# Placing w_down's stationary operands at two residues modulo 256 bytes

## The chip, the cores and the metric

One core of a Trainium2 chip runs the whole program. The metric is the device time of one execution in microseconds (us). Each number below comes from the runs of the kernel before, from the profile of one execution of it, or from the addresses that the program's allocator gives to its tiles.

## The reference, cut to what matters

One layer of a decoder on 256 positions of width 1024, all float32. First a mixer of three attention branches, then a gated channel mixer ("the MLP half"), on which the change bears:

```python
h2 = rmsnorm(x, ln2)
u = causal_dwconv(h2 @ w_up, conv_w, conv_b)   # w_up: 1024 x 5632
a, b = jnp.split(u, 2, axis=-1)
return x + (jax.nn.silu(a) * b) @ w_down       # w_down: 2816 x 1024
```

A final RMSNorm with weight `ln_f` follows.

## The kernel before, in words

**Products in three parts.** Each float32 operand of a large product is split into a high part (rounded to the type float32r) and a low part (what the rounding left), and a product is the sum of three matmuls: high by high, low by high, high by low. `mm3` (line 241) issues them in this order for a stationary operand `lhs` and a moving operand `rhs`: `lh` with `rh` (line 243), `ll` with `rh` (line 244), `lh` with `rl` (line 245). Each matmul brings its own load of 128 stationary columns, which TensorE's load queue (PEld in the profile) works on while the matmul before it runs.

**Weights.** `Weights` (line 56) streams the weight pieces of 128 x 1024 from memory by the SP queue, in the order of use, into five raw buffers. Its step "hi" (line 109, ScalarE) makes `whi`, its step "lo" (line 116, VectorE) `wlo`. Six buffers of each lie in the pool `wpool`, and four more of each in the pool `mlp` during the MLP half.

**The MLP half** (from line 882) runs over j = 0 to 21, 128 channels of each half of `u` at a time. For each j:

- two w_up products, `up` (line 850) and `up_mm` (line 830), 24 matmuls each: the weights are the stationary operand, `h2T` (the normed input, transposed, 128 x 256 per step) is the moving one; line 834 issues all of them. Their results go to the PSUM banks `s0` and `s1` for even j, `pt` and `o` for odd j;
- `conv_of` (line 837) on VectorE and ScalarE for each of the two, SiLU (line 889), the product `pr` (line 894), and its split into `ah` (line 901) and `al` (line 902), each 128 x 256;
- from j = 2 on, save j = 9 and 16, one w_down product for an older j, `down` (line 823): `ah` and `al` are stationary, 128 columns at a time, and `whi` and `wlo` of w_down are moving, 512 wide. It is four calls of `mm3`, so 12 matmuls. `downs_after` (line 43) gives the plan: d = 0 at j = 2 up to d = 17 at j = 21. The last four d (18 to 21) come behind the loop, and the last columns of them in matmuls 256 wide.

The instructions stand in each engine's queue in the order in which the code issues them (`manual_schedule`), so the order on TensorE is: w_up, w_up, w_down, w_up, w_up, w_down, and so on. `ah` and `al` have a ring of six buffers each (`TAIL + 2`), so that slot j % 6 is written again six steps later.

**Names in the profile.** A group such as `acc<-whi,ah` names the output bank, the moving operand and the stationary operand in this order. `h2T` has the buffers of the earlier `oThi` and `oTlo`, so w_up reads `s<-oThi,whi`: moving `h2T` high, stationary `whi`. A PSUM tag's number is left out, so `s` is `s0` and `s1`.

**Addresses.** Modulo 256 bytes, within a partition:

| tile | where it is used | residue |
|---|---|---|
| `whi`, `wlo`, all ten buffers of each | stationary in w_up, moving in w_down, in w_o, in the branch projections | 64 |
| `oThi`, `oTlo` (later `h2T`) | stationary in the branch projections (`project`, line 701), moving in w_up | 0 |
| `hThi`, `hTlo` (later `mT`) | stationary in w_o (`wo_mm`, line 740) and in the row products of the attention half (`row_piece`, line 398), moving in `qk_piece` (line 378) | 64 |
| `v`, `ya`, `yb`, `pr` | the conv and its product | 64 |
| `ah`, `al`, six buffers of each | stationary in w_down | 64 |

Steps inside these tiles are multiples of 512 bytes, but for the row products 260 wide, so the residue of a tile is that of its slices.

Of the kernel before, what the change touches and what calls it, by code (L numbers as in the profile page):

```python
# [7 lines left out]
F32 = mybir.dt.float32  # L8
F32R = mybir.dt.float32r
# [3 lines left out]
P = 128  # L13
S = 256
# [18 lines left out]
TAIL = 4  # L33
# [9 lines left out]
def downs_after():  # L43

    out, d = [], 0
    for j in range(NF):
        if j >= 2 and j not in PAUSES:
            out.append(d)
            d += 1
        else:  # L50
            out.append(None)
    assert d == NF - TAIL
    return out
# [86 lines left out]
def hybrid_kernel(ctx: ExitStack, tc: tile.TileContext, x, xT, ln_f, w_main, w_v1, w_v2, b_f, sinks,  # L140
# [22 lines left out]
    def piece(lead=LEAD):  # L163
        nxt[0] += 1
        return W.use(nxt[0] - 1, lead, 1)
# [81 lines left out]
    def small(shape, name, bufs=2):  # L247
        return act.tile([P] + shape, F32, name=name, tag=name, bufs=bufs)
# [439 lines left out]
    ml = ctx.enter_context(tc.tile_pool(name="mlp", bufs=1))  # L688
# [124 lines left out]
    def up_banks(j):  # L813
        return [bank(tag, S) for tag in (("s0", "s1"), ("pt", "o"))[j % 2]]
# [8 lines left out]
    def down(j, parts):  # L823
        if not zo:
            zo.extend([bank("acc", 512, 4) for _ in range(2)] for _ in range(2))
        for t in range(2):
            for half in range(2):
                down_mm(j, t, half * 512, half * 512 + 512, parts)
# [8 lines left out]
    def conv_of(u, f, name):  # L837
        v = ml.tile([P, S], F32, name="v", tag="v", bufs=4)
        nc.vector.tensor_mul(v, u, rs["row2"])  # L839
        y = ml.tile([P, S], F32, name=name, tag=name, bufs=3)  # L840
        w = [cv[:, i * 2 * NF + f:i * 2 * NF + f + 1] for i in range(4)]
        nc.scalar.activation(y, v, AF.Identity, scale=w[2], bias=w[3])  # L842
        ahead()
        nc.vector.scalar_tensor_tensor(y[:, 1:S], v[:, 0:S - 1], w[1], y[:, 1:S],
                                       op0=OP.mult, op1=OP.add)
        nc.vector.scalar_tensor_tensor(y[:, 2:S], v[:, 0:S - 2], w[0], y[:, 2:S],
                                       op0=OP.mult, op1=OP.add)
        return y

    def up(j, c, u):  # L850
        parts = piece(0)
        for k in range(KD):
            up_mm(u, parts, k)

    def up_first(u):
        parts = [piece(0), piece(0)]
        for c in range(2):
            for k in range(4):
                up_mm(u[c], parts[c], k)
            if c == 0:  # L860
                low = h2_T(*blocks[-1], "pt")
                low()
                squares(*blocks[-1])
        rs["row2"], *finish = across(rstd_of(ss2[:, :, 0], ss2[:, :, 1], "n"), "row2", "acc", 4)
        ahead()
        for some in ((0, 1), (2,)):
            for k in range(4, KD):
                up_mm(u[0], parts[0], k, some)
        for k in range(4, KD):
            up_mm(u[1], parts[1], k)  # L870
        for f in finish:
            f()
        ahead()
        nc.scalar.preload_act_table_set("silu_and_others")

    def ahead():
        n = HL_BUFS + MORE_BUFS - 2
        W.prep_to(min(nxt[0] + n - 1, W.n_lo + 1))
        W.hi_to(min(nxt[0] + n, W.n_hi + 1))

    downs = downs_after()
    for j in range(NF):
        u = up_banks(j)
        if j == 0:
            up_first(u)
        else:
            up(j, 0, u[0])
        ya = conv_of(u[0], j, "ya")
        nc.scalar.activation(ya, ya, AF.Silu)
        if j:  # L890
            up(j, 1, u[1])
        yb = conv_of(u[1], j + NF, "yb")
        pr = ml.tile([P, S], F32, name="pr", tag="pr", bufs=3)
        nc.vector.tensor_mul(pr, ya, yb)
        hi = ml.tile([P, S], F32R, name="ah", tag="ah", bufs=TAIL + 2)
        lo = ml.tile([P, S], F32R, name="al", tag="al", bufs=TAIL + 2)
        d = downs[j]
        if d is not None:
            parts = piece(0)
            ahead()  # L900
        nc.scalar.activation(hi, pr, AF.Copy)
        nc.vector.tensor_sub(lo, pr, hi.bitcast(F32))
        mid[j] = (hi, lo)
        if d is not None:
            down(d, parts)
# [51 lines left out]
    v, r = (small([1], n) for n in ("fv", "fr"))  # L957
# [88 lines left out]
```

## Time and profile before

| | us |
|---|---|
| median of 3 runs | 388.01 (387.05 to 389.1) |
| the profiled execution | 388.68 |
| its span, first to last instruction | 387.0 |

The mean granted TensorE clock of the profiled execution is 0.993 of full speed. In the profile, PE is TensorE's matmuls, PEld its weight loads, DVE VectorE, ACT ScalarE, POOL GpSimd, SP the queue of SyncE that issues the transfers. The chain of work that ended last is followed back from the last instruction; in its list each entry has a start, a length and, for merged instructions of one line, their count. Matmuls overlap in their pipeline, so the "mean ns" of one in a group is longer than the distance from one start to the next; the distance is what the chain's lengths show, and it is what time is made of on TensorE.

### The profile page before, as it was taken

To read this page: it belongs to the slowest core of one execution; us is meant where nothing else is said; L and a number is where in the kernel's file an instruction comes from. 1 tells how busy PE (TensorE), PEld (TensorE's weight loads), DVE (VectorE), ACT (ScalarE), POOL (GpSimd) and SP (SyncE) were. 2 spreads that over 40 slices of the span, in tenths; PEclk is the share of its full clock that TensorE was granted. 3 is DMA by queue.
4 is the path that set the end of the run, shared out by engine and by line. 5 is a ranking of instruction groups with operands and counts; after the bars stand their busy time and mean duration, and the time that the engine had idled before them with its cause. 6 is when DMAs were issued, how large, how long until landed. Compare 5 with 4: busy or idle time off the path is not lost.

```text
span 387.0 us, 6530 instructions
## 1 busy us (share of the span) xinstructions
PE 377.2 (97%) x2464; PEld 340.1 (88%) x2464; DVE 287.7 (74%) x540; ACT 230.7 (60%) x399; POOL 8.0 (2%) x20
## 2 busy tenths in 40 slices
PE   6999999999999999999999999999999999999993
PEld 6999999787887888888899999999999999999983
DVE  3785967574856717967778999878887878888745
ACT  4883464665757685336587767556655656656433
POOL 4010000000000000000000000000000000000000
PEclk9899999999999999999999999999999999999998
DMA  7999765344552637444736567655565556463002
GB/s 197 402 331 334 279 181 181 130 130 149 170 172 90 218 108 233 151 160 119 262 108 222 204 224 223 216 196 186 170 213 180 201 171 205 171 218 109 2 0 108
DMA packets 21374, 70.86 MB, mean 183 GB/s; under 512 B 2504, under 2 KB 3413, under 8 KB 21344
## 3 DMA queue, kind: packets, MB, share of 16 engines
q1 hardware_dynamic: 20448, 68.05, 52.1%
q0 software_dynamic: 752, 2.18, 1.7%
q8 instruction: 19, 0.31, 0.4%
q10 hardware_dynamic: 144, 0.23, 0.2%
q14 instruction: 11, 0.09, 0.1%
HBM read 69.38 MB, written 1.07 MB: 182 GB/s over the span
## 4 chain that ended last, share of the span: by engine, by line
PE 96%; DMA 1%; DVE 1%; SPq 0%; ACT 0%; issue 0%; DVEq 0%
PE s L834 16%; PE acc L243 16%; PE acc L244 15%; PE acc L245 15%; PE pt L834 8%; PE o L834 8%; PE acc L394 7%; PE pt L394 2%; PE s L619 2%; PE o L394 1%; DMA raw<-in_w_main 1%; PE s L566 1%; PE s L608 1%; PE s L301 0%; PE pt L566 0%; PE pt L773 0%
## 5 line engine op out<-in xcount | busy, mean ns | idle before, releaser
L116 DVE TENSOR_TENSOR wlo<-raw,whi 128x1024 fp32r<-128x1024 f32 (+4 forms) x131 | 150.3, 1161 | 17.4 <-ACT whi L109 17.4
L109 ACT ACTIVATE whi<-raw 128x1024 fp32r<-128x1024 f32 (+4 forms) x131 | 129.1, 1005 | 49.2 <-PE acc L244 24.6
L243 PE MATMUL acc<-whi,hThi 128*128 128x512 f32 (+2 forms) x160 | 61.3, 383 | 0.0
L244 PE MATMUL acc<-whi,hTlo 128*128 128x512 f32 (+2 forms) x160 | 59.8, 374 | 0.0
L245 PE MATMUL acc<-wlo,hThi 128*128 128x512 f32 (+2 forms) x160 | 59.8, 374 | 0.0
L834 PE MATMUL s<-oThi,whi 128*128 128x256 f32 x176 | 49.3, 281 | 0.0
L834 PE MATMUL s<-oThi,wlo 128*128 128x256 f32 x176 | 49.2, 280 | 0.0
L834 PE MATMUL s<-oTlo,whi 128*128 128x256 f32 x176 | 48.9, 280 | 0.0
L842 ACT ACTIVATE ya<-v,cv 128x256 f32<-128x256 f32 x22 | 13.3, 603 | 42.7 <-DVE v L839 42.7
L243 PEld LDWEIGHTS acc<-whi,hThi 128*128 128x128 f32 x160 | 30.1, 188 | 6.0 <-issue 1.3
L245 PEld LDWEIGHTS acc<-wlo,hThi 128*128 128x128 f32 x160 | 30.0, 188 | 5.1
L244 PEld LDWEIGHTS acc<-whi,hTlo 128*128 128x128 f32 x160 | 30.1, 188 | 4.7 <-DVE hTlo L295 0.2
L244 PE MATMUL acc<-whi,al 128*128 128x512 f32 (+1 forms) x88 | 33.8, 384 | 0.0
L245 PE MATMUL acc<-wlo,ah 128*128 128x512 f32 (+1 forms) x88 | 33.8, 384 | 0.0
L243 PE MATMUL acc<-whi,ah 128*128 128x512 f32 (+1 forms) x88 | 33.8, 384 | 0.0
L834 PEld LDWEIGHTS s<-oTlo,whi 128*128 128x128 f32 x176 | 33.5, 191 | 0.0
L834 PEld LDWEIGHTS s<-oThi,wlo 128*128 128x128 f32 x176 | 33.0, 188 | 0.4
L834 PEld LDWEIGHTS s<-oThi,whi 128*128 128x128 f32 x176 | 33.0, 188 | 0.4
L834 PE MATMUL pt<-oThi,whi 128*128 128x256 f32 x88 | 24.8, 282 | 0.0
L834 PE MATMUL pt<-oThi,wlo 128*128 128x256 f32 x88 | 24.7, 281 | 0.0
L834 PE MATMUL pt<-oTlo,whi 128*128 128x256 f32 x88 | 24.7, 281 | 0.0
L834 PE MATMUL o<-oThi,whi 128*128 128x256 f32 x88 | 24.7, 281 | 0.0
(243 smaller groups left out, 749.0 us busy)
## 6 DMA issues: line engine op xcount, KB each, us to landing
raw<-in_w_main SPq DMA_DIRECT2D x115, 512.0 KB, 3.8
raw<-in_w_main SPq DMA_DIRECT2D x7, 256.0 KB, 5.6
raw<-in_w_v SPq DMA_DIRECT2D x4, 384.0 KB, 3.9
xt<-in_x SPq DMA_DIRECT2D x2, 512.0 KB, 6.9
G<-rowsd POOLq DMA_DIRECT2D x1, 1024.0 KB, 12.6
raw<-in_w_v SPq DMA_DIRECT2D x2, 390.0 KB, 6.2
G<-in_xT SPq DMA_DIRECT2D x3, 256.0 KB, 6.1
out_y<-xt SPq DMA_DIRECT2D x2, 288.0 KB, 2.2
```

What stands on the lines that cost most here:

```text
L109: self.nc.scalar.activation(self.parts[i][0][:, cs], self.raw[i][:, cs], AF.Copy)
L116: self.nc.vector.tensor_sub(lo[:, cs], self.raw[i][:, cs], hi[:, cs].bitcast(F32))
L243: nc.tensor.matmul(o, lh, rh, start=start, stop=False, **kw)
L244: nc.tensor.matmul(o, ll, rh, start=False, stop=False, **kw)
L245: nc.tensor.matmul(o, lh, rl, start=False, stop=stop, **kw)
L394: nc.tensor.matmul(o, w[:, kk, cs], hT[h][:, k, :], start=first, stop=last, skip_group_check=True)
L566: nc.tensor.matmul(sc[2 * i + e][:, lo:lo + m], q[h, qi, qs], k[h, ki, 0:m], start=True, stop=True)
L608: nc.tensor.transpose(pts[h][:, i * P:(i + 1) * P], L[:, h, i * P:(i + 1) * P], ident)
L619: nc.tensor.matmul(os[i][e * HD:(e + 1) * HD, cs], v[t][:, vi, e, :], p[:, S:ROWS] if t else p[:, 0:S], start=t == 0, stop=t == 1, **kw)
L834: nc.tensor.matmul(u, w, h2T[h][:, k, :], start=k == 0 and i == 0, stop=k == KD - 1 and i == 2)
L842: nc.scalar.activation(y, v, AF.Identity, scale=w[2], bias=w[3])
```

## The change: two residues for the stationary operands of w_down

Before the loop over j, twelve tiles get buffers of their own, `ah0` to `ah5` and `al0` to `al5`, where there were two rings of six. They are allocated in two groups. The first six, from the place where the pool stands at that point (residue 64), are `al0` to `al4` and `ah5`. Then a tile `gap` of 48 floats (192 bytes), which nothing uses, moves the pool to residue 0. The other six follow there: `ah0` to `ah4` and `al5`. In step j, slot j % 6 is used, as in the ring before. So for five of six slots the high part lies at 0 and the low part at 64, and for the sixth slot (j = 5, 11, 17) the other way round.

```diff
+    places = [(0, 64)] * (TAIL + 1) + [(64, 0)]
+
+    def act_parts(j):
+        i = j % len(places)
+        return [ml.tile([P, S], F32R, name=n, tag=n, bufs=1) for n in ("ah%d" % i, "al%d" % i)]
+
+    for r in (64, 0):
+        for i, place in enumerate(places):
+            for n, at_r in zip(("ah", "al"), place):
+                if at_r == r:
+                    ml.tile([P, S], F32R, name=n + str(i), tag=n + str(i), bufs=1)
+        if r:
+            ml.tile([P, 48], F32, name="gap")
+
     downs = downs_after()
     for j in range(NF):
...
         pr = ml.tile([P, S], F32, name="pr", tag="pr", bufs=3)
         nc.vector.tensor_mul(pr, ya, yb)
-        hi = ml.tile([P, S], F32R, name="ah", tag="ah", bufs=TAIL + 2)
-        lo = ml.tile([P, S], F32R, name="al", tag="al", bufs=TAIL + 2)
+        hi, lo = act_parts(j)
```

The tiles `v`, `ya`, `yb` and `pr` are first asked for inside the loop, so they are allocated behind the two groups now and lie at residue 0.

## The prediction, made before the change was run

> **What bounds the kernel now.** I read the page first (busy shares, then the chain that ended last), then the waits of TensorE, then the chain piece by piece, and last the groups by form and the timeline around the first w_down product.
>
> ```profile
> span 387.0 us, 6530 instructions
> ...
> PE 377.2 (97%) x2464; PEld 340.1 (88%) x2464; DVE 287.7 (74%) x540; ACT 230.7 (60%) x399; POOL 8.0 (2%) x20
> ...
> PE 96%; DMA 1%; DVE 1%; SPq 0%; ACT 0%; issue 0%; DVEq 0%
> ```
>
> ```profile
> engine line waited for: us in total, times, longest us
> PE pt L394 <- ACT whi L109: 1.7, 1, 1.7
> PE s L199 <- DVE warm L196: 1.1, 1, 1.1
> PE pt L394 <- DVE wlo L116: 0.2, 1, 0.2
> PE s L619 <- DVE nm L578: 0.2, 1, 0.2
> ```
>
> TensorE is busy for 97% of the span and is 96% of the chain. Its waits stand in lines of the attention half alone (L199, L394, L619): in the MLP half nothing holds it up. So an edit there is worth what it does to the distance from one matmul to the next, and nothing else. Adding no instruction and removing none, the change can act only through that distance.
>
> In the chain each matmul counts as long as the distance to the next:
>
> ```profile
> 148.59 0.23 PE acc L243
> ...
> 157.52 0.23 PE acc L243
> ...
> 194.28 0.24 PE acc L243
> 194.52 0.23 PE acc L244
> 194.75 0.24 PE acc L245
> 194.99 0.23 PE acc L243
> ...
> 202.16 2.73 PE pt L834 x24
> 204.89 2.72 PE o L834 x24
> 207.61 5.44 PE s L834 x48
> ...
> 215.78 2.83 PE pt L834 x24
> 218.61 2.83 PE o L834 x24
> 221.44 0.23 PE acc L243
> ...
> 224.16 5.65 PE s L834 x48
> ...
> 277.33 0.23 PE acc L243
> ...
> 280.05 2.83 PE pt L834 x24
> 282.88 2.83 PE o L834 x24
> ...
> 352.69 5.65 PE s L834 x48
> ```
>
> The reader is to see one thing here above all. The w_up products (L834) are the same 48 matmuls of the same shape for every j, on tiles of the same residues, with no wait between them, and yet they take 5.44 us for j=2 and 5.65 us from j=3 on: 113.3 ns each against 117.7. The change of pace comes exactly at the first w_down product, which ends at 215.78 (the two pieces of j=3 take 2.83 each, those of j=1 took 2.73 and 2.72). From there to the last j the slow pace never goes away. The pace is not in the data or in the engines around, then, but in how the stream of weight loads stands to the stream of matmuls, and a w_down product hands that on to the w_up products behind it.
>
> The timeline shows the hand-over:
>
> ```profile
> 212.77 0.28 PE L834 MATMUL s<-oTlo,whi 128*128 128x256 f32 x1
> 212.89 0.39 PE L243 MATMUL acc<-whi,ah 128*128 128x512 f32 x1
> 213.12 0.40 PE L244 MATMUL acc<-whi,al 128*128 128x512 f32 x1
> 213.35 0.39 PE L245 MATMUL acc<-wlo,ah 128*128 128x512 f32 x1
> 213.58 0.39 PE L243 MATMUL acc<-whi,ah 128*128 128x512 f32 x1
> ```
>
> Coming from the fast pace, the first three matmuls of the first w_down product take 0.69 us together (212.89 to 213.58), 230 ns each. All later products sit at another figure: twelve matmuls from 277.33 to 280.05 are 226.7 ns each. So with all operands at 64 the w_down stream slides into one fixed spacing within three matmuls and leaves the w_up stream behind it always at the same point.
>
> **The change part by part.**
>
> *Instructions, waits, memory.* The slots keep their ring of six: slot j % 6 is written again six products later, as before. No instruction, DMA or queue entry is added. The gap costs 192 bytes of a partition. Cost: nothing.
>
> *Vector and scalar operands.* The conv tiles v, ya, yb and pr are now allocated behind the gap and come to lie at 0 modulo 256 as well, and so does the high slot that line 901 writes.
>
> ```profile
> L902 DVE TENSOR_TENSOR al<-pr,ah 128x256 fp32r<-128x256 f32 x22 | 9.2, 420 | 2.5 <-ACT ah L901 2.5
> ...
> L627 DVE TENSOR_TENSOR oTlo<-s,oThi 128x256 fp32r<-128x256 f32 x8 | 3.2, 420 | 8.9 <-ACT oThi L624 8.8
> ```
>
> The subtraction of line 902 works on tiles at 64 and takes 420 ns; that of line 627, the same shape, reads and writes SBUF tiles at 0 and takes 420 too. I put this edit at nothing. What hides it in any case is the up product of the next half (2.83 us a piece) that TensorE has before it. If that cover went, a stall of TensorE on ah or al would be in its waits, where no line of the MLP stands now.
>
> *The w_down stream itself.* It has 22 products of 12 matmuls, 264, nearly all 512 wide. Their moving operands whi and wlo lie at 64. Before, the stationaries lie at 64 too: 226.7 ns. After, two of three stationaries lie at 0 (one of three in the sixth slot). The nearest rows with moving at 64 and stationaries at 0 are the branch projections, whose oThi and oTlo lie at 0: from 148.59 to 157.52 there are 13 turns of L243, L244 and L245, so 39 matmuls in 8.93 us, 229.0 ns each. That is 2.3 ns more, times 264: +0.6 us. As the dear bound I take three matmuls of w_o that stand right behind four transposes and so out of the fixed spacing: 194.28 to 194.99, 236.7 ns each, 10 ns times 264: +2.6 us. As the cheap bound, the step between the two paces of L834, 4.4 ns a matmul (moving at 0, stationary at 64): -1.2 us. I take +0.6, the row with these residues.
>
> The Trainium skill (TensorE: Matmul & The Clock Gate, "Back-to-back issue gap") puts a 512-wide matmul at about 215.7 ns; by that the w_down stream could gain up to an estimated 2.9 us. The rows above, 226.7 and 229.0, stand against it.
>
> *The w_up stream behind it.* From j=3 to j=21 there are 19 times 48 matmuls. Each j at the fast pace saves 5.65 - 5.44 = 0.21 us; all of them save 4.0 us. The fast pace holds itself: j=1 and j=2 run in it for 96 matmuls without a drift (2.73, 2.72, 5.44). The change takes away the fixed spacing in which every product ended at the same point. Where the projections show no such spacing, I expect the w_down stream with mixed residues to end at other points, some of which lie in the fast pace; once there, the same product at the same slot pattern hands it on. The two reversed products that have w_up behind them (d=5 and d=11) I let fall back to the slow pace for one j each. That leaves 17 times 0.21: -3.6 us.
>
> *Sum.* -3.6 + 0.6 = -3.0 us. On the profiled execution (388.68 us, of which 387.0 are span and 1.7 lie around it) that is 385.7. The median of the runs shown is 388.01, 0.7 below the profiled one; on it the forecast is **385.0 us**. About 0.5%, 1.9 us, is what a measurement of this kernel can tell from no change.
>
> **The rivals.**
>
> *A: the slow pace stays.* The products end at other points than before, but all or most of these are in the slow pace. For it: of the two paces the slow one follows every hand-over from a 512-wide stream in this trace, and the fast one appears first behind the change of j=0 to j=1. Against it: the 17 hand-overs from w_down are one and the same case, a fixed spacing at 226.7, so they count as one. Time: 388.0 + 0.6 = 388.6. If half of the 19 run fast, -2.0 + 0.6, 386.6: still within 0.5%.
>
> *B: the address does nothing.* Then the whole change is without effect: 388.0. For it stands only that the w_down and w_o rows and the row products of before agree with each other. Against it: projections at 229.0 where w_down has 226.7, the same shape on other residues. The Trainium skill (the same page, "Step-by-step: what each phase is for") states this rule: TensorE reads moving operand and weights through two independent ports, so that loading the next weights takes nothing from the running matmul. The trace does not bear it out as far as the pace goes: 113.3 and 117.7 ns for the same matmuls.
>
> *C: slower.* The w_down stream loses its fixed spacing and gets none in exchange, so that each matmul pays what the three of w_o pay, 236.7 ns, and w_up stays slow: +2.6 us, 390.6. It decides from 234 ns a matmul on (7.3 ns times 264 is 1.9 us). For it: any break of the stream in this trace is followed by some matmuls over 230. Against it: the projections, out of the fixed spacing for 39 matmuls on end, average 229.0.
>
> **How the numbers follow.** The forecast has 0.47. Rival A in its two forms has 0.32, B 0.09, C 0.12. So faster by over 0.5%: 0.47; within: 0.41; slower: 0.12. I lean to the forecast because the slow pace of j=3 to j=21 hangs on one fixed point, and the change breaks just that. The forecast's own range runs from all 19 fast with the w_down stream 0.4 us cheaper (388.0 - 4.4 = 383.6, a third of the cheap bound) to 13 fast and +0.8 (386.1). The range over all cases leaves out C and the little that lies lower: 383.6 to 388.8.
>
> **What would show it.** In the chain of the changed kernel, w_up entries of 48 at 5.44 us behind w_down products say that the main step is right, and those at 5.65 say that A holds. Twelve w_down matmuls should take some 2.75 us (229 ns each); 2.72 would speak for B, 2.84 for C. The waits of TensorE should still name no line of the MLP. The prediction is wrong if w_up keeps 5.65 throughout, or if it is faster with w_up at 5.65, which would put the gain into w_down, where I see none.

## The result and the profile after

| | before | changed |
|---|---|---|
| median, us | 388.41 (387.05 to 389.1, 7 runs) | 385.72 (384.25 to 386.23, 7 runs) |
| span of the profiled execution, us | 387.0 | 384.5 |
| mean granted clock | 0.993 | 0.991 |

The ratio is 0.9939 with a 95% interval from 0.992 to 0.9958: 2.7 us faster by the medians; the ratio, 0.6%, makes it 2.4.

The page of the changed kernel, its first lines and its chain by engine, looks as before; nothing new waits, and the waits of TensorE still name the lines of the attention half alone:

```profile
span 384.5 us, 6530 instructions
...
PE 374.7 (97%) x2464; PEld 336.7 (88%) x2464; DVE 288.0 (75%) x540; ACT 230.9 (60%) x399; POOL 7.7 (2%) x20
...
PE 96%; DMA 1%; DVE 1%; SPq 0%; ACT 0%; issue 0%; DVEq 0%
```

```profile
PE pt L394 <- ACT whi L109: 1.8, 1, 1.8
PE s L199 <- DVE warm L196: 1.1, 1, 1.1
PE pt L394 <- DVE wlo L116: 0.2, 1, 0.2
PE s L619 <- DVE nm L578: 0.2, 1, 0.2
```

The chain of the changed kernel, piece by piece (start, length, engine and bank, line, count), shows where the time came from:

```profile
195.42 1.42 PE s L834 x12
197.27 4.13 PE s L834 x36
201.84 2.83 PE pt L834 x24
204.67 2.83 PE o L834 x24
207.50 5.65 PE s L834 x48
215.95 2.73 PE pt L834 x24
218.67 2.72 PE o L834 x24
224.14 5.47 PE s L834 x48
...
257.01 5.66 PE s L834 x48
265.45 2.73 PE pt L834 x24
268.17 2.72 PE o L834 x24
270.89 5.44 PE s L834 x48
...
311.95 2.83 PE pt L834 x24
314.78 2.83 PE o L834 x24
320.39 5.45 PE s L834 x48
...
```

Three things are to be seen. From the first w_down product on, w_up runs at the fast pace: 5.44 to 5.47 us for a j, where before it had 5.65. Two j from 3 on are slow, those at 257.01 (j=8) and at 311.95 (j=15): they stand right behind the products of d=5 and d=11, the reversed slots. And here j=1 (2.83 and 2.83) and j=2 (5.65) are slow, which before were fast, though no operand of TensorE in front of them was moved.

The chain around the first product, in the changed kernel, shows what w_down pays for it:

```profile
213.15 0.24 PE acc L243
...
221.40 0.23 PE acc L243
...
224.14 0.93 PE s L834 x8
```

The product of d=0 comes from a slow j and takes 2.80 us for its twelve matmuls (213.15 to 215.95), 233 ns each; the product of d=1 comes from a fast j and takes 2.74 (221.40 to 224.14), 228 to 229 each. Before, they took 2.73 and 2.72 (213.05 to 215.78, 277.33 to 280.05).

The sum, from starts in the two chains: w_up of j=3 to 21 loses 3.3 us; j=0 to 2, from the first w_up entry to the first w_down product, take 17.73 where they took 17.37, +0.4; the 17 w_down products between get 0.6 longer; that is -2.3 from the first w_up entry (195.68 before, 195.42 after) to the end of the last (366.72 and 364.13). The rest of the 2.5 us of span lies ahead of w_up, -0.3, and behind it, +0.1. The 0.3 ahead is there at the 66 matmuls of line 394 already, which start at 27.68 (27.98 before), so it comes from the start of the program and not from the change.

### The profile page after: what moved, and what is told of

The parts are those of the page before. It is cut to its first block, busy times and chain, and to the rows that moved or that the text cites. A ratio compares the mean times of both kernels' runs of the same rounds, so it can differ in the third digit from the quotient of the medians.

```text
span 384.5 us, 6530 instructions
## 1 busy us (share of the span) xinstructions
PE 374.7 (97%) x2464; PEld 336.7 (88%) x2464; DVE 288.0 (75%) x540; ACT 230.9 (60%) x399; POOL 7.7 (2%) x20
## 4 chain that ended last, share of the span: by engine, by line
PE 96%; DMA 1%; DVE 1%; SPq 0%; ACT 0%; issue 0%; DVEq 0%
PE acc L243 16%; PE s L834 16%; PE acc L244 15%; PE acc L245 15%; PE pt L834 8%; PE o L834 8%; PE acc L394 7%; PE pt L394 2%; PE s L619 2%; PE o L394 1%; DMA raw<-in_w_main 1%; PE s L566 1%; PE s L608 1%; PE s L301 0%; PE pt L566 0%; PE pt L773 0%
## 5 line engine op out<-in xcount | busy, mean ns | idle before, releaser
L834 PE MATMUL o<-oTlo,whi 128*128 128x256 f32 x88 | 24.4, 277 | 0.0
```

The source lines that it names most:

```text
L834: nc.tensor.matmul(u, w, h2T[h][:, k, :], start=k == 0 and i == 0, stop=k == KD - 1 and i == 2)
```

## The experiments

The figures "beside" which a time stands are those of the kernel before on the same chip. The edits are shown against the changed kernel, unless another is named. The theory tested is the one of the prediction: the point at which a w_down product ends decides the pace of the w_up products behind it. Its rivals are that the conv operands do it, that any mixture of residues does, and that the reversed slot is needed.

### The conv tiles alone

All twelve slots at 64, with buffers of their own, and the gap behind them:

```diff
-    places = [(0, 64)] * (TAIL + 1) + [(64, 0)]
+    places = [(64, 64)] * (TAIL + 2)
```

> All twelve slots lie at 64 as before, in buffers of their own, with the gap behind them, so that of all that the change does only the move of v, ya, yb and pr to 0 and the buffers of their own are left. Theory (only the stationary operands matter): 388.4 as before, w_down at 226.7 ns a matmul, w_up slow from j = 3 on. Rival (the operands of the vector and scalar engines collide with TensorE's reads less at 0 than at 64): about 385.7, w_up at 113.3 ns.

Measured: 387.62 us beside 387.53, ratio 0.9995 (0.9977 to 1.0014). Its chain has 2.83 and 5.65 from j=3 on:

```profile
...
239.12 5.65 PE s L834 x48
247.50 2.83 PE pt L834 x24
250.32 2.83 PE o L834 x24
...
```

The move of `v`, `ya`, `yb` and `pr` and the buffers of their own are worth nothing; the stationary operands are the change.

### All slots one way, all slots the other way

```diff
-    places = [(0, 64)] * (TAIL + 1) + [(64, 0)]
+    places = [(0, 64)] * (TAIL + 2)
```

> All six slots have the high part at 0 and the low part at 64. Theory (the pace of w_up is handed on by the w_down product before it, and a product with high at 0 and low at 64 hands on the fast pace): the two j behind the reversed slots, slow in the changed kernel at 5.42 us for 48 matmuls, become fast, 5.24; every j from 3 on is fast; about 0.4 us below the changed kernel, 385.3 beside a before of 388.4. Rival (the reversed slot is needed, since without it the run settles into another fixed spacing): w_up is slow at some or all j from 3 on and the time lies between 386 and 388.6.

Measured: 384.18 us beside 387.53, ratio 0.9905 (0.9882 to 0.9928); 3.35 us below by the medians, where 3.1 was expected. (The expectation's 5.42 and 5.24 fit twice the 23 distances from the first to the last start of 24 matmuls; they are the 5.65 and 5.44 to 5.47 of the chains, which count all 48.) Every j from 3 on is fast; the j that was slow in the changed kernel behind d=5 is the first line here, the one behind d=11 the last two:

```profile
256.65 5.47 PE s L834 x48
...
311.37 2.75 PE pt L834 x24
314.12 2.72 PE o L834 x24
```

The reversed slot is not needed. The other way in all slots:

```diff
-    places = [(0, 64)] * (TAIL + 1) + [(64, 0)]
+    places = [(64, 0)] * (TAIL + 2)
```

> All six slots have the high part at 64 and the low part at 0. Theory (the order of the residues within a product decides where it ends): as behind the reversed slots of the changed kernel, w_up stays slow, 2.71 us for 24 matmuls, at most or all j from 3 on, and w_down costs about 230 ns a matmul: 388.4 + 0.8, about 389. Rival (any mixture of two residues breaks the fixed spacing and gives the fast pace): about 385.5.

Measured: 388.99 us beside 387.53, ratio 1.0022 (1.0003 to 1.004). No j from 3 on is fast, though j=1 and 2 came in fast:

```profile
...
249.32 2.83 PE pt L834 x24
252.14 2.83 PE o L834 x24
257.74 5.65 PE s L834 x48
```

The product between 252.14 + 2.83 and 257.74 takes 2.77 us, 231 ns a matmul. The same mixture in the other order brings only the cost: the rival by which any mixture frees w_up falls.

### All slots at 0

```diff
-    places = [(0, 64)] * (TAIL + 1) + [(64, 0)]
+    places = [(0, 0)] * (TAIL + 2)
```

> All twelve slots lie at 0. Theory (the end point of a product depends on the residues of all its weight loads): w_down takes about 229 ns a matmul, as the branch projections do with stationaries at 0 and moving at 64; whether w_up is fast I cannot derive, since no w_up follows a projection: 385.3 if it is, 389.0 if not. Rival (the relation does not matter, only that not all operands share a residue): w_up fast, 385.3.

Measured: 384.18 us beside 387.53, ratio 0.9906 (0.9879 to 0.9932), every j fast (5.47 at 239.17 for j=6, and so on), w_down at 228 to 229 ns a matmul, as the projections have it. So no mixture is needed either. This settles nothing about the theory by itself, since both outcomes were open, but it is the simplest form of the gain. One thing can be read from the four placements at 0 and 64 together: the pace of w_up goes with the high part alone. With `ah` at 0 it is fast, wherever `al` lies, and with `ah` at 64 it is slow. `ah` is the stationary operand of two of every three matmuls, of the last one of a product too; which of these loads counts was not tested apart.

### All slots at 128, and at 192

Here a gap stands ahead of the twelve slots, which all lie behind it: 16 floats for 128, as shown, and 32 for 192.

```diff
-    places = [(0, 64)] * (TAIL + 1) + [(64, 0)]
+    ml.tile([P, 16], F32, name="gap")
...
+    for i in range(TAIL + 2):
+        act_parts(i)
```

> All twelve slots lie at 128, so that the weight load of a w_down matmul stands 64 above its moving operand, as in w_up (moving 0, stationary 64). Theory (what counts is the distance of the two residues and the end point): w_down itself can take a spacing below 226.7 ns, down to 222 if it gains what the two paces of w_up differ by; 264 times 4.7 ns is 1.2 us; with w_up fast that is about 383, with w_up slow 387. Rival (only residue 0 of the stationary operands is good, whatever the distance): w_down 226.7 or above, w_up slow, 388.

> All twelve slots lie at 192, 128 above the moving operands. Theory (end point): no fixed spacing at 226.7 as with equal residues, so w_up comes into the fast pace or not by where the product ends; the two times are 384.5 and 388.5, and I cannot say which. Rival (any residue but that of the moving operand gives the fast pace): 384.5.

Measured: 387.84 us for 128 (ratio 1.0004, 0.9988 to 1.002) and 387.02 for 192 (0.999, 0.9974 to 1.0006), beside 387.48. With 128, fast and slow j take turns, behind one product each:

```profile
239.69 5.46 PE s L834 x48
247.94 2.83 PE pt L834 x24
250.77 2.83 PE o L834 x24
256.40 5.46 PE s L834 x48
264.65 2.83 PE pt L834 x24
267.48 2.83 PE o L834 x24
270.30 5.66 PE s L834 x48
278.76 2.74 PE pt L834 x24
```

With 192 they take turns as well:

```profile
251.48 2.83 PE o L834 x24
257.09 5.45 PE s L834 x48
265.31 2.83 PE pt L834 x24
```

With 128 the product from 250.77 + 2.83 to 256.40 takes 2.80 us, 233 ns a matmul, and with 192 the one from 251.48 + 2.83 to 257.09 takes 2.78, 231 to 232: dearer than with equal residues. So most of what the fast half of the j saves goes to the products, and the time stays within 0.1% of the kernel before. My hope that a load 64 above its moving operand would be cheaper for w_down is wrong, and the rival of the second run, that any other residue will do, is wrong too. The other rival, that only residue 0 is good, has its time (388) but not its chain: half of the j are fast. Behind a fast j and its product comes a slow one, and the other way round: here the pace that comes in counts too, and not only that the residues were changed.

### The end point by itself

If the moment decides, all residues may stay as before. In the kernel before, one additional matmul is put between each w_down product and the w_up products behind it, 17 in all. The banks of w_up are asked for with 512 columns in place of 256, and the matmul writes columns of them that nothing reads (the diff is against the kernel before). The 6.67 ns of the expectation is a step of which the paces in the chains are whole multiples: 226.7 is 34 of them, 113.3 is 17.

```diff
     def up(j, c, u, full):
         parts = piece(0)
+        if c == 0 and downs[j - 1] is not None:
+            nc.tensor.matmul(full[:, S:S + 192], parts[0][:, 0:P], h2T[0][:, 0, 0:192],
+                             start=True, stop=True, skip_group_check=True)
...
```

> The kernel before with all operands at 64, and one additional matmul, 192 columns wide, between each w_down product and the w_up products behind it (17 in all, its result is not used). Theory (the pace of w_up hangs on the moment at which the w_down product ends, taken modulo 6.67 ns, since the starts of the fixed w_down spacing fall on one residue of it): the added 111 ns or so end in the slow part; w_up stays at 2.71 us for 24, time 388.0 + 17 x 0.11 = 389.9. Rival (any break of the stream behind w_down frees w_up): w_up fast at 2.61 to 2.63, time about 386.5.

> The same with the additional matmul 194 columns wide, 0.8 ns longer. Theory: this puts the start of w_up into the fast part; w_up takes 2.61 to 2.63 us for 24 behind each product, 19 x 0.2 = 3.8 us come off and 17 x 0.11 = 1.9 us are added: about 386.1, faster than before by adding work, and 3.8 us faster than with 192 columns. Rival (the end point is not what decides): both widths take the same time.

Measured: with 192 columns 385.83 us, ratio 0.9949 (0.9932 to 0.9966); with 194 columns 390.0 us, ratio 1.0057 (1.0038 to 1.0076), both beside 387.48. The chain with 192 columns:

```profile
240.98 5.48 PE s L834 x48
249.29 2.76 PE pt L834 x24
252.05 2.72 PE o L834 x24
```

and with 194:

```profile
240.69 5.67 PE s L834 x48
249.19 2.85 PE pt L834 x24
252.04 2.83 PE o L834 x24
```

Two columns, by the pace of 113.3 ns for 256 an estimated 0.9 ns, in 17 places turn the whole w_up stream from one pace to the other and move the time by 4.2 us. With 192 the kernel does more work than before and is faster. So the pace can be switched with every residue left as it was. But the theory had forecast the reverse, 192 slow and 194 fast, and that the moment decides is not shown by two widths: 192 columns of four bytes are 768 bytes, three times 256, and 194 are 776, so the length of the read tells the two runs apart as well as the time does. Further widths were not run. The timeline of the run with 192 shows one thing that my count had wrong.

```profile
224.12 0.25 PE L853 MATMUL s<-oThi,whi 128*128 128x192 f32 x1
224.21 0.30 PE L834 MATMUL s<-oThi,whi 128*128 128x256 f32 x1
224.35 0.28 PE L834 MATMUL s<-oThi,wlo 128*128 128x256 f32 x1
```

I had taken some 111 ns for the additional matmul; it takes 90 (224.12 to 224.21) and the one behind it 140, so the two starts fall elsewhere than I had put them. Whether a count with these figures names the right width was not worked out. The rival of the first (any break helps) falls with the second run, and that of the second (both widths take the same time) with both.

### Once more, and a further operand

> The changed kernel once more, beside the two without a reversed slot on the same chip. Theory (the reversed slots cost the j behind them): slow w_up at j = 8 and j = 15 alone, if j = 1 and 2 come in fast this time; between 0.4 and 0.8 us above the other two. Rival (which j are slow is chance of the run): other j are slow than in the first profile.

> All six slots with high at 0 and low at 64, a second time. Theory: every j from 3 on fast again, 384.2, some 0.5 us below the changed kernel. Rival (its first figure was luck of the chip): as the changed kernel.

> All slots at 0, a second time. Theory: as the kernel with 0 and 64 in all slots, within 0.1%: both hand on the fast pace and both pay 229 ns a w_down matmul. Rival (a mixture is worth something by itself): slower than that one by over 0.3 us.

Measured, beside 387.5: the changed kernel 385.16 us, 0.9931 (0.9911 to 0.9951); all slots at 0 and 64, 384.18, 0.99 (0.9881 to 0.992); all at 0, 383.75, 0.9899 (0.9881 to 0.9917). In the second profile of the changed kernel j=8 (5.66 us from 255.70) and j=15 (2.83 from 310.64) are slow again, j=1 and 2 too. In the second profile of the kernel with 0 and 64 throughout, j=1 and 2 are slow (2.83 from 200.72), which were fast in its first (2.74 from 201.94). So which pace j=1 and 2 get is chance of the execution, worth 0.4 us; the two j behind the reversed slots belong to the kernel and cost 0.2 us each. By the medians the version without reversed slots is about 1 us better than the changed kernel; the intervals overlap, so that only the two slow j, 0.4 us of it, are shown. (0.4 to 0.8 between them was expected.) Some of the 1 us goes with the granted clock: three of the six executions of the changed kernel had 0.991 and took 385.4 us or more, the other three had at least 0.994 and took 384.2 to 384.9, and all five of the other kernel had at least 0.995. Between (0, 64) and (0, 0) nothing can be told apart.

Last, the operands of the attention half were moved in the same way, with all slots of w_down at 0. The second pad brings what lies behind it back to its old residue; some small tiles between the two pads move along:

```diff
+    act.tile([P, 48], F32, name="pad3")
     hT = [act.tile([P, KD, S], F32R, name=n, tag=n, bufs=1) for n in ("hThi", "hTlo")]
...
-    act.tile([P, 16], F32, name="pad1")
+    act.tile([P, 32], F32, name="pad1")
```

> All slots at 0, and hThi and hTlo too moved from 64 to 0 by a pad. They are the moving operand of the 312 matmuls of line 394, which sit at 120 ns with both operands at 64, and the stationary one of 480 matmuls of the row products and of w_o. Theory: line 394 comes to one of the two paces of w_up, 113.3 or 117.7 ns, which saves 2.1 or 0.7 us; the other 480 go from 226.7 to 229, as the projections have it, which costs 1.1; together 1.0 below to 0.4 us above the kernel with all slots at 0. Rival (the residue works in the MLP half alone): no difference to that kernel.

Measured: 383.36 us, ratio 0.9885 (0.9865 to 0.9905), the lowest median of all. Line 394 (395 here) with all slots at 0 alone, in its second run, and with `hThi` and `hTlo` at 0 too:

```profile
26.13 7.90 PE acc L394 x66
...
193.88 1.42 PE s L834 x12
```

```profile
25.80 7.49 PE acc L395 x66
...
192.97 1.38 PE s L835 x12
```

66 matmuls take 7.49 us where they took 7.90: 113.5 ns against 119.7. The effect is not one of the MLP half alone. The 0.4 us between the two medians is within the forecast of the theory, but the intervals overlap, so the sum of gain (line 394) and loss (row products with stationaries at 0) is not shown by the times to be a gain. In these two executions w_up starts 0.9 us earlier with `hThi` and `hTlo` at 0 (192.97 against 193.88), 0.3 of which is there by the first lines shown; j=1 and 2 came in slow in that one (2.83 from 199.35), which takes back 0.4.

## Why the prediction was right, point by point

**The bound.** TensorE without a wait in the MLP half: as the prediction had it, and still so after.

**The main step.** That w_up takes the fast pace behind products with mixed residues was forecast with 17 of 19 j and 3.6 us. Measured: 17 of 19 and 3.3 us. The two that fall back, behind d=5 and d=11, are the ones named, and with all slots that way round every j from 3 on is slow. What was left out is an entry: behind a product the first piece takes 2.75 us and not 2.72 (5.47 and not 5.44 for a j), 25 ns for twelve of the j, together 0.3 us. The prediction could not derive where the changed products end; it spoke of "other points, some of which lie in the fast pace". That the placement chosen was one that brings it was luck in part: of the five placements run, (0, 64) and (0, 0) have the fast pace behind every product, (64, 0) behind none, 128 and 192 behind every other one. And the prediction had a product hand on the pace once the stream is in it. With high at 0 and low at 64 the product sets it: those of d=0, 6 and 12 come from a slow j, and the j behind them, from 215.95, 265.45 and 320.39, are fast.

**w_down.** Forecast 229.0 ns a matmul from the projections, +0.6 us for all 22 products. Measured 228 to 233 by product, +0.6 for the 17 up to the last w_up and some 0.1 more for those behind it. The row with the same residues was the right one to take, and the dear bound, 236.7, was not reached by a whole product. The products behind a slow j (233) are what was missing in the term.

**The conv tiles.** Forecast at nothing, shown to be nothing (0.9995).

**The rivals.** A (slow pace stays) is what happens with the residues the other way round, 388.99 where A had 388.6 (by the ratio 0.9 us above the kernel before, where A had 0.6). B (the address does nothing) is refuted: the same w_up matmuls take 113.3 or 117.7 ns on nothing but other residues of w_down's stationaries. The Trainium skill (TensorE: Matmul & The Clock Gate, "Step-by-step: what each phase is for") says that loading the next weights takes no read bandwidth from the running matmul. As far as the distance between matmuls goes, these runs do not bear that out: w_down with its moving operands at 64 took 226.7 ns a matmul with the stationary ones at 64, 228 to 229 at 0, 231 to 232 at 192 and 233 at 128. Whether the load or the matmul is held up in it was not seen. C (slower) did not come.

**What the prediction did not have.** The pace of j=1 and 2 is chance, +0.4 us in the profiled execution. It had read their fast pace in one trace as a property of the kernel. The 0.3 us that the start of the program was shorter is chance too, so that the two nearly cancel: from -3.0, the entries (0.3), w_down (0.1) and these two (0.4 and -0.3) lead to the -2.5 of the span.

**What stays open.** That the residues of w_down's stationary operands set the pace of w_up is shown; by what way is not. That it goes by the moment at which the product ends is argued, and the runs with 192 and 194 columns fit it only after the event. The steady spacings of the chains are close to whole multiples of 6.67 ns (113.3 is 17, 226.7 is 34, 119.7 about 18 of them, and three matmuls at the slow pace of 117.7 are 53), which would fit starts that are bound to a grid of that step. The 229.0 of the projections fits only by threes (687 is 103 of them), and no run shows the grid itself.

## What to carry to other kernels

Where TensorE never waits and the same matmuls still take two different times in one trace, compare the distance between starts group by group, in order of time: the pace of a stretch may be set by the stretch before it. Then try the address residues of stationary and moving operands (the gap of 192 bytes cost nothing here: 0.9995 with the conv tiles alone), look at each j and not at the mean, and undo every part that is not needed: here the reversed sixth slot cost 0.4 us, and one residue for all slots did as well as two.

## What the runs showed of the hardware

A stream of weight load and matmul pairs has more than one stable spacing for the same shape and addresses: 113.3 or 117.7 ns for 256 columns with moving at 0 and stationary at 64, 119.7 with both at 64, 113.5 with moving at 0 in line 394. It keeps the one that it comes into, for 48 matmuls and more. Two columns more or less in one matmul at 17 places decided between the two and were worth 4.2 us of 388. A 512-wide matmul with its moving operand at 64 took 226.7 ns with the stationary one at 64, 228 to 229 at 0, and 231 to 233 at 128 and 192.
